# Mixture-of-experts stage: two kinds of experts take turns by column block, three experts of the first kind instead of four

## The chip, the cores and the metric

The kernel runs on one core of one Trainium2 chip. The metric is device time in microseconds (us): the time of one execution. Times of runs without a profile are compared with each other; the trace comes from one profiled execution, whose own time stands beside its span.

## The reference, cut to what matters

The program is two transformer blocks one after the other, 256 tokens of width 1024 in fp32. Around the change stands one mixture-of-experts layer with 8 experts of which each token takes 2:

```python
logits = h @ router_w                      # 256 x 8
top_val, top_idx = top_k(logits, 2)
gates = softmax(top_val)
for each expert e, for the tokens that chose it:
    y = (silu(x @ w1[e]) * (x @ w3[e])) @ w2[e]     # w1, w3: 1024 x 2816, w2: 2816 x 1024
    out[token] += gate * y
```

The weights of one expert are 3 x 1024 x 2816 fp32 numbers, 34.6 MB; all eight are read whole. With the inputs that are used here the routing gives 79 tokens to expert 0 and 109, 96, 58, 48, 42, 41 and 39 to the others in falling order (the reference, evaluated).

## The kernel before, in words

`moe` (L1117) routes the tokens, sorts experts 1 to 7 by their number of tokens (expert 0 keeps the first place, so that its weights can be loaded before the routing is known) and treats the first `NL` = 4 places and the other 4 differently.

**First kind, "three products"** (places 0 to 3): up to 128 tokens each. Every weight chunk is split into a rounded part `hi` (ScalarE, ACT, L325) and the rest `lo` (VectorE, DVE, L326), the tokens likewise, and TensorE (PE) adds three products `hi*hi`, `hi*lo`, `lo*hi` (L1370 for w1 and w3, L1436 for w2).

**Second kind, "plain"** (places 4 to 7): up to 64 tokens each. The weight chunks go to PE as fp32, unsplit (L1387 for w1 and w3, L1450 for w2), two products side by side on the two halves of 64 columns.

Weights come as *chunks* of 1 MB, each as two DMAs of 512 KB on SyncE's (SP's) queue (L310), 33 chunks an expert. The order of the stream is the order of the steps. A **step** `(e, f)` is one column block of an expert: 6 blocks of 512 columns for the first kind (the last has 256), 3 pairs of blocks for the second. `moe_steps` (L58) lists the steps: all of the four first-kind experts, then all of the four plain ones. For each step `moe` (L1501) emits `up(step)` (w1 and w3), inside it between w1 and w3 the transposes `gtrans` of the step before (L1408 or L1417, into PSUM and copied out), and then `down(step before)` (w2). After each one or two chunks `tick` lets a piece of background work come (gathers of the next tokens, L1298 and L1328; `combine` and `combine_plain`, L1456 and L1477, which scatter an expert's result into the residual `hT`) and `pump` loads and splits ahead.

**Buffers.** A chunk needs a place from one of the `home`s (L273). Between 454 and 847 us there are 6 (3 `raw`, 2 `raw2`, 1 `raw3`), and at the start 3 extra ones that are used once (`xbig` twice, `yh`/`yl`). A split chunk gives its place back as soon as the split is emitted; at most `look` = 2 split chunks wait ahead of their use, and `hi` and `lo` have room for 3 chunks. In the plain part the six places of `hi` and `lo` serve as homes as well (L631 to L634), so that there are 12; `may_split` (L344) holds splits back while they do. A plain chunk gives its place back in `done`, after its products (a pair of chunks in `up`, one in `down`).

**PSUM.** Eight banks: 3 for `mm` (the sums `H` and others), 1 `st`, 2 `Y` (the sums of w2), 2 `ac` (all that is short-lived: `gTp` of `gtrans`, gathers, `sc` of the combines).

A second path, `moe_rest` (L1523), handles experts with more tokens than their slots; it runs only where `ovm` (L1221 to L1223) exceeds 128, counting 64 on top for the plain places.

Of the kernel before, what the change touches and what calls it, by code (L numbers as in the profile page):

```python
# [23 lines left out]
NL = 4  # L24
# [33 lines left out]
def moe_steps():  # L58

    return [(e, f) for e in range(NL) for f in range(6)] + [(e, f) for e in range(NL, NE) for f in range(3)]  # L60

# [117 lines left out]
class Prog:  # L179
# [74 lines left out]
    def plan(self):  # L254
# [13 lines left out]

        self.i_plain = self.at_key["m1", NL, 0, 0], self.i_raw2

        self.i_three = self.at_key[down_keys(NL - 1, 5)[-1]]

    def home(self, pool, chunks, tag="raw", ok=lambda i: True):  # L273

        r = dict(pool=pool, free=chunks, tag=tag, ok=ok)
        self.homes.append(r)
        return r
# [16 lines left out]
    def _load(self):  # L294
# [5 lines left out]
        else:  # L300
# [7 lines left out]
            r = [home["pool"].tile([128, n, shape[2]], F32, tag=home["tag"], name=f"raw{i}{h}") for h in range(2)]  # L308
# [316 lines left out]
    def setup(self):  # L625
# [491 lines left out]
    def moe(self, nxt):  # L1117
# [117 lines left out]
        def gates():  # L1235
# [13 lines left out]
            for b in range(2):  # L1249
# [7 lines left out]
        io64 = p.tile([128, 2, 64], F32, name="io64")  # L1257
        nc.gpsimd.iota(io64, pattern=[[0, 2], [1, 64]], base=0, channel_multiplier=0,
                       allow_small_or_imprecise_dtypes=True)
        io64 = io64.rearrange("p a b -> p (a b)")  # L1260


        def slots(es, off=0, io=io8):
            S = p.tile([128, 2, len(es), 128], F32R, tag="ST" if off else "S", name="S", bufs=2 if off else 1)
            for n, e in enumerate(es):
                for b in range(2):
                    if off:
                        nc.vector.tensor_scalar(S[:, b, n], io, float(off), rks[:, b, e:e + 1], op0=OP.add,
                                                op1=OP.is_equal)
                    else:  # L1270
                        nc.vector.tensor_scalar(S[:, b, n], io, rks[:, b, e:e + 1], None, op0=OP.is_equal)
            return S

        def slotsT(S, es, ghl):

            m = len(es)
            ST = p.tile([128, m, T], F32R, tag="ST", name="ST", bufs=2)
# [5 lines left out]
            gs = p.tile([128, m, 2], F32, tag="gs", name="gs", bufs=2)  # L1283
# [10 lines left out]
        first = slots((0, 1))  # L1294
# [3 lines left out]
        def gather(pair):  # L1298
            es = (2 * pair, 2 * pair + 1)
            S = slots(es) if pair else first  # L1300
            last = [None, None]
            if pair % 2:
                g = [self.big("xgh", [128, KD, 2, 128], F32R), self.big("xgl", [128, KD, 2, 128], F32R)]
            else:
                g = [self.xt(n).rearrange("p k (e t) -> p k e t", e=2) for n in ("xgh", "xgl")]
            for i in range(4):
                for s in range(2):
                    ps = self.psum("ac" if s or pair else "mm", "xgp", (128, 2, 256))
                    for j in range(2):
                        for b in range(2):  # L1310
                            k = 2 * i + j
                            nc.tensor.matmul(ps[:, j], xtk[k // 4][:, s, b, 128 * (k % 4):128 * (k % 4) + 128], S[:, b],
                                             start=b == 0, stop=b == 1)
                    o = g[s][:, 2 * i:2 * i + 2].rearrange("p a b c -> p a (b c)")
# [5 lines left out]
            if not pair:  # L1320
                with self.after(*last):
                    ghl.append(gates())
            q = slotsT(S, es, ghl[0])
            for n, e in enumerate(es):
                xg[e] = [x[:, :, n] for x in g]
                sg[e] = q[0][:, n], q[1][:, n]

        def gather_plain():  # L1328

            es = range(NL, NE)  # L1330
            n = len(es)
            S = slots(es, io=io64)
            yield
            g = self.p_x.tile([128, KD, n, 64], F32, tag="X", name="xs")
            for k in range(KD):
                ps = self.ac("xgp", (128, n, 64))
                for s in range(2):
                    for b in range(2):
                        nc.tensor.matmul(ps, xtk[k // 4][:, s, b, 128 * (k % 4):128 * (k % 4) + 128], S[:, b, :, 0:64],
                                         start=s == 0 and b == 0, stop=s == 1 and b == 1)  # L1340
                if k % 2:
# [816 lines left out]
```

## Time and profile before

| | |
|---|---|
| three runs | 1894.77 us median, 1893.84 to 1897.97 |
| the profiled execution | 1895.51 us, its span 1893.7 us |
| granted TensorE clock over the span | 0.985 |
| busy over the span | PE 95%, DVE 66%, ACT 52%, POOL 3% |
| share of the chain that ended last | PE 49%, DMA 18%, DVE 6%, ACT 2% |

The span runs from the first to the last instruction. In what follows the *first stage* is 454 to 847.4 us (experts with three products) and the *second stage* 847.4 to 1184.2 us (plain experts); both are in the middle of the span, behind the first block's mixer and feed-forward layer and ahead of the second block. Busy PE time is modelled, so a stage's PE share is read together with what PE waited for.

### The profile page before, as it was taken

To read this page: it belongs to the slowest core of one execution; us is meant where nothing else is said; L and a number is where in the kernel's file an instruction comes from. 1 tells how busy PE (TensorE), PEld (TensorE's weight loads), DVE (VectorE), ACT (ScalarE), POOL (GpSimd) and SP (SyncE) were. 2 spreads that over 40 slices of the span, in tenths; PEclk is the share of its full clock that TensorE was granted. 3 is DMA by queue.
4 is the path that set the end of the run, shared out by engine and by line. 5 is a ranking of instruction groups with operands and counts; after the bars stand their busy time and mean duration, and the time that the engine had idled before them with its cause. 6 is when DMAs were issued, how large, how long until landed. Compare 5 with 4: busy or idle time off the path is not lost.

```text
span 1893.7 us, 32031 instructions
## 1 busy us (share of the span) xinstructions
PE 1789.7 (95%) x11975; PEld 1474.0 (78%) x11975; DVE 1255.5 (66%) x2216; ACT 975.8 (52%) x1503; POOL 55.4 (3%) x94
## 2 busy tenths in 40 slices
PE   6999999997999999999888988799999999999998
PEld 6999999996888887873232322788899999889997
DVE  6789888687999888971000100786788887676554
ACT  6754336666787777761000000666655556666553
POOL 1010000000000000000000000110100000000000
PEclk9999999998999999999999999899999999999999
DMA  7478886664899999999999999644388884326551
GB/s 254 163 254 323 306 315 211 207 249 161 301 363 328 349 329 354 326 335 392 411 411 411 411 411 411 205 130 143 133 281 318 313 277 145 109 78 200 181 189 54
DMA packets 138547, 508.57 MB, mean 269 GB/s; under 512 B 18192, under 2 KB 18832, under 8 KB 137872
## 3 DMA queue, kind: packets, MB, share of 16 engines
q1 hardware_dynamic: 132768, 497.97, 72.9%
q10 hardware_dynamic: 5616, 8.48, 1.4%
q8 instruction: 96, 1.57, 0.3%
q14 instruction: 67, 0.55, 0.1%
HBM read 505.34 MB, written 1.05 MB: 267 GB/s over the span
## 4 chain that ended last, share of the span: by engine, by line
PE 49%; DMA 18%; DVE 6%; ACT 2%; issue 2%; SPq 0%; DVEq 0%; ACTq 0%
DMA raw<-in_moe_dram 16%; PE H L1370 10%; PE up L406 8%; PE y L603 8%; PE zp L406 5%; PE Y L1436 5%; DVE lo L326 3%; PE H L1387 3%; PE op L406 2%; PE S L1780 1%; DMA adaw<-in_ada_dram 1%; ACT hi L325 1%; PE pg L406 1%; PE pTp L998 1%; PE oT L1814 1%
## 5 line engine op out<-in xcount | busy, mean ns | idle before, releaser
L326 DVE TENSOR_TENSOR lo<-raw,hi 128x1024 fp32r<-128x1024 f32 x580 | 695.1, 1224 | 135.6 <-ACT hi L325 133.1
L325 ACT ACTIVATE hi<-raw 128x1024 fp32r<-128x1024 f32 x580 | 589.8, 1052 | 166.0 <-PE y L603 37.2
L1387 PE MATMUL H<-raw,xs 128*64 128x512 f32 (+1 forms) x768 | 189.6, 574 | 29.9 <-DMA raw<-in_moe_dram 29.8
L603 PE MATMUL y<-glo,hi 128*128 128x256 f32 x688 | 193.4, 281 | 1.3 <-DVE glo L378 1.3
L603 PE MATMUL y<-ghi,hi 128*128 128x256 f32 x688 | 193.2, 281 | 0.6 <-ACT ghi L377 0.6
L603 PE MATMUL y<-ghi,lo 128*128 128x256 f32 x688 | 193.3, 281 | 0.2 <-DVE lo L326 0.2
L1397 DVE SCALAR_TENSOR_TENSOR mg<-H,gs,mg 128x512 f32<-128x512 f32 (+3 forms) x40 | 27.8, 695 | 237.8 <-PE H L1387 138.1
L1387 PEld LDWEIGHTS H<-raw,xs 128*64 128x64 f32 x768 | 61.3, 139 | 146.7 <-issue 76.1
L828 DVE SCALAR_TENSOR_TENSOR adacc<-adaw,cact,adacc 128x768 f32<-128x768 f32 x126 | 130.3, 1034 | 42.4 <-DMA adaw<-in_ada_dram 40.8
L1396 ACT ACTIVATE mg<-H,gs 128x512 f32<-128x512 f32 (+3 forms) x40 | 25.7, 643 | 255.9 <-PE H L1387 239.7
L406 PE MATMUL up<-xhi,hi 128*128 128x258 f32 x512 | 145.6, 285 | 2.4 <-ACT xhi L481 1.8
L1370 PE MATMUL H<-hi,xgh 128*128 128x512 f32 (+1 forms) x384 | 145.8, 380 | 0.0
L406 PE MATMUL up<-xlo,hi 128*128 128x258 f32 x512 | 145.6, 284 | 0.1
L406 PE MATMUL up<-xhi,lo 128*128 128x258 f32 x512 | 145.1, 284 | 0.0
L1370 PE MATMUL H<-lo,xgh 128*128 128x512 f32 (+1 forms) x384 | 144.8, 377 | 0.3
L1370 PE MATMUL H<-hi,xgl 128*128 128x512 f32 (+1 forms) x384 | 143.5, 374 | 0.0
L603 PEld LDWEIGHTS y<-glo,hi 128*128 128x128 f32 x688 | 129.6, 188 | 2.1 <-DVE glo L378 2.1
L603 PEld LDWEIGHTS y<-ghi,hi 128*128 128x128 f32 x688 | 129.3, 188 | 1.2 <-ACT ghi L377 1.2
L603 PEld LDWEIGHTS y<-ghi,lo 128*128 128x128 f32 x688 | 129.6, 188 | 0.6 <-DVE lo L326 0.6
L406 PE MATMUL H<-xhi,hi 128*128 128x256 f32 x352 | 99.3, 283 | 2.3 <-ACT xhi L481 2.3
L406 PE MATMUL H<-xhi,lo 128*128 128x256 f32 x352 | 100.1, 285 | 0.7 <-DVE lo L326 0.7
L1450 PE MATMUL Ys<-raw,gts 128*64 128x512 f32 x352 | 94.4, 606 | 6.6 <-DMA raw<-in_moe_dram 5.9
(552 smaller groups left out, 4017.2 us busy)
## 6 DMA issues: line engine op xcount, KB each, us to landing
raw<-in_moe_dram SPq DMA_DIRECT2D x522, 512.0 KB, 6.4
raw<-in_stream_dram SPq DMA_DIRECT2D x318, 512.0 KB, 4.6
adaw<-in_ada_dram SPq DMA_DIRECT2D x64, 768.0 KB, 6.3
xbig<-in_moe_dram SPq DMA_DIRECT2D x4, 512.0 KB, 5.3
cw1k<-in_cw1k_dram ACTq DMA_DIRECT2D x2, 1024.0 KB, 6.2
cw1v<-in_cw1v_dram ACTq DMA_DIRECT2D x2, 1024.0 KB, 6.7
raw<-in_stream_dram SPq DMA_DIRECT2D x4, 472.0 KB, 4.2
hT<-in_xT_dram SPq DMA_DIRECT2D x4, 256.0 KB, 6.1
```

Of the source, the lines that this page charges most:

```text
L325: nc.scalar.activation(hi, raw, AF.Copy)
L326: nc.vector.tensor_sub(lo, raw, hi.bitcast(F32))
L406: nc.tensor.matmul(ps, p[:, k, j:j + m], q[:, k, :], start=start and n == 0, stop=n == 3 * nk - 1, skip_group_check=True)
L603: self.nc.tensor.matmul(ps, p[:, k, 128 * dt:128 * dt + 128], q[:, k, :], start=f == 0 and n == 0 and dt % 2 == 0, stop=last and n == 5, s ...
L828: nc.vector.scalar_tensor_tensor(acc, w[:, j], self.cact[:, k:k + 1], acc, op0=OP.mult, op1=OP.add)
L998: nc.tensor.transpose(ps[:, o:o + 128], e[:, c:c + 128], self.ident)
L1370: nc.tensor.matmul(ps[:, :n], g[s][:, m // 3], w[:, k], start=m == 0, stop=m == 23, skip_group_check=True)
L1387: nc.tensor.matmul(ps[64 * q:64 * q + 64, :c], g[:, k], x[:, kk], start=k == 0, stop=k == KD - 1, skip_group_check=True)
L1396: nc.scalar.activation(t[z, :c], H[0][z, :c], AF.Silu, scale=gs[z, 1:2])
L1397: nc.vector.scalar_tensor_tensor(t[z, :c], H[1][z, :c], gs[z, 1:2], t[z, :c], op0=OP.mult, op1=OP.mult)
L1436: nc.tensor.matmul(Y[e][q], l[:, kk], r[:, k, 512 * q:512 * q + 512], start=f == 0 and h == 0 and k == 0 and i == 0, stop=f == 5 and k == ...
L1450: nc.tensor.matmul(Y[e][64 * q:64 * q + 64], gt[:, kk, 64 * n:64 * n + 64], w[:, k, 512 * q:512 * q + 512], start=key[2] == 0 and kk == 0, ...
```

## The change

`NL` becomes 3, so places 3 to 7 are plain. `moe_steps` gives first three steps of the first kind and then one plain step and one of the first kind by turns; the last plain step but one is followed by two of the first kind, and a plain step ends the list. There are 18 + 15 = 33 steps (24 + 12 before). The plain tokens are gathered in two groups (three and two experts) that are queued at once after the first step, and each first-kind expert's tokens one expert ahead. The homes in `hi` and `lo` go; `raw3` has two chunks instead of one, and one `xbig` instead of two. PSUM has `Y` = 3 and `ac` = 1; the plain combine uses one `ac` and one `mm` bank instead of two `ac`. A combine is queued when the last step of its expert is done.

```diff
-NL = 4
+NL = 3
...
 def moe_steps():
-    return [(e, f) for e in range(NL) for f in range(6)] + [(e, f) for e in range(NL, NE) for f in range(3)]
+    a = [(e, f) for e in range(NL) for f in range(6)]
+    b = [(e, f) for e in range(NL, NE) for f in range(3)]
+    r, n = a[:3], 3
+    for i, x in enumerate(b):
+        r.append(x)
+        m = 3 + (len(a) - 3) * (i + 1) // (len(b) - 1)
+        r += a[n:m]
+        n = max(n, m)
+    assert r[-1] == b[-1] and len(r) == len(a) + len(b)
+    return r
...
     def may_split(self):
-        if self.i_split not in self.raws or self.plain(self.i_split):
-            return self.i_split in self.raws
-        return len([i for i in self.parts if not self.plain(i)]) < self.look and \
-            not any(x["tag"] != "raw" and x["free"] < x["all"] for x in self.homes if "all" in x)
+        return self.i_split in self.raws and (
+            self.plain(self.i_split) or len([i for i in self.parts if not self.plain(i)]) < self.look)
...
-        for pool, tag in ((self.p_hi, "hi"), (self.p_lo, "lo")):
-
-            self.home(pool, self.look + 1, tag, lambda i: self.i_get > self.i_three + 1 and i < self.i_plain[1] - 6)
-            self.homes[-1]["all"] = self.look + 1
...
-        for _ in range(2):
-            t = self.big("xbig", [128, 2048])
-            self.extra.append([t[:, 0:1024], t[:, 1024:2048]])
+        t = self.big("xbig", [128, 2048])
+        self.extra.append([t[:, 0:1024], t[:, 1024:2048]])
...
-        first = slots((0, 1))
+        first = slots((0,))
...
-        def gather(pair):
-            es = (2 * pair, 2 * pair + 1)
-            S = slots(es) if pair else first
+        def gather(e):
+            S = slots((e,)) if e else first
...
+            g = self.p_x.tile([128, 2, KD, 128], F32R, tag="X", name="xg")
+            for i in range(2):
                 for s in range(2):
...
+                    for j in range(4):
                         for b in range(2):
...
         def gather_plain():
-            es = range(NL, NE)
...
+            g = self.big("xs", [128, KD, NE - NL, 64])
+            for e0 in range(NL, NE, 3):
+                es = range(e0, min(e0 + 3, NE))
...
-                P = [self.ac("sc", (128, 2, T)) for _ in range(2)]
+                P = [self.psum(t, "sc", (128, 2, T)) for t in ("ac", "mm")]
...
             up(e, f, prev)
-            if e < NL and e % 2 and f == 1:
-                self.add(gather(e // 2 + 1) if e < NL - 1 else gather_plain())
+            if n == 0:
+                self.add(gather_plain())
+            if e < NL - 1 and f == 1:
+                self.add(gather(e + 1))
             if prev:
                 down(*prev)
-                if f == 0:
-                    self.add((combine if e <= NL else combine_plain)(e - 1))
+                if prev == (prev[0], 5 if prev[0] < NL else 2):
+                    self.add((combine if prev[0] < NL else combine_plain)(prev[0]))
...
-        with self.more_raw("raw3", "left", 1), self.phase("moe", 2, Y=2, ac=2):
+        with self.more_raw("raw3", "left", 2), self.phase("moe", 1, Y=3, ac=1):
```

## Rows read from the trace of the kernel before

**Rows 1.** The page's 40 slices of the span, 47.3 us each

```profile
PE   6999999997999999999888988799999999999998
...
DMA  7478886664899999999999999644388884326551
GB/s 254 163 254 323 306 315 211 207 249 161 301 363 328 349 329 354 326 335 392 411 411 411 411 411 411 205 130 143 133 281 318 313 277 145 109 78 200 181 189 54
```

**Rows 2.** Busy time by stretch: first stage, second stage, first three steps

```profile
core 0: us, PE busy (x) PEld busy (x) DVE busy (x) ACT busy (x) POOL busy (x), PEclk, DMA share, GB/s
454.00:847.40 393.40, 392.82 (x1895) 322.56 (x1894) 350.35 (x365) 292.89 (x329) 0.12 (x1) 1.00 0.93 333
847.40:1184.20 336.80, 295.92 (x1250) 98.17 (x1248) 32.98 (x52) 16.92 (x25) 0.11 (x1) 0.99 1.02 406
454.00:503.00 49.00, 49.00 (x221) 39.86 (x220) 44.79 (x60) 39.16 (x43) 0.00 (x0) 1.00 0.76 268
```

**Rows 3.** DMA issues of expert weights, 452.2 to 1190 us

```profile
raw<-in_moe_dram SPq DMA_DIRECT2D x506, 512.0 KB, 6.6
```

**Rows 4.** Busy time by stretch: one short stretch of each stage

```profile
650.00:653.00 3.00, 3.00 (x16) 2.45 (x15) 2.24 (x2) 1.10 (x2) 0.00 (x0) 1.00 1.03 419
980.00:1000.00 20.00, 17.88 (x82) 6.96 (x82) 1.42 (x3) 1.15 (x2) 0.00 (x0) 1.00 1.03 411
```

**Rows 5.** SP's queue waits, first stage, then second: us, times, longest

```profile
SPq L310 <- DVE lo L326: 239.3, 235, 10.1
...
SPq L310 <- DMA raw<-in_moe_dram: 182.6, 243, 1.6
```

**Rows 6.** Splits; landing of weight DMAs, first stage, then second

```profile
L326 DVE TENSOR_TENSOR lo<-raw,hi x252: 1209/1219/1228, 443.1 to 845.6; 128x1024 fp32r<-128x1024 f32 x126
...
L325 ACT ACTIVATE hi<-raw x251: 1038/1053/1067, 439.7 to 843.4; 128x1024 fp32r<-128x1024 f32 x126
...
DMA to landing us min/median/max: 3.2/5.3/7.2
...
DMA to landing us min/median/max: 3.5/10.1/11.3
```

**Rows 7.** The page's groups, then groups by line: PE, second kind

```profile
L1387 PE MATMUL H<-raw,xs 128*64 128x512 f32 (+1 forms) x768 | 189.6, 574 | 29.9 <-DMA raw<-in_moe_dram 29.8
...
L1450 PE MATMUL Ys<-raw,gts 128*64 128x512 f32 x352 | 94.4, 606 | 6.6 <-DMA raw<-in_moe_dram 5.9
...
L1490 PE MATMUL sc<-ST,ys 64*128 64x256 f32 x64 | 11.7, 407 | 1.6 <-ACT ys L1482 0.8 <-DVE hT L1493 0.8
...
L1417 PE MATMUL gTp<-ident,mg 128*128 128x128 f32 (+1 forms) x48 | 8.9, 286 | 2.6 <-DVE hT L1493 2.3
```

**Rows 8.** Timeline: products of the second kind around one combine product

```profile
880.06 0.14 PEld L1387 LDWEIGHTS H<-raw,xs 128*64 128x64 f32 x1 [0.29 <-issue]
881.01 0.19 PEld L1472 LDWEIGHTS sc<-ST,yl 128*128 128x128 f32 x1 [0.81 <-issue]
...
881.32 0.20 PEld L1387 LDWEIGHTS H<-raw,xs 128*64 128x64 f32 x4
...
881.80 0.14 PEld L1387 LDWEIGHTS H<-raw,xs 128*64 128x64 f32 x2 [0.28 <-issue]
882.24 0.14 PEld L1387 LDWEIGHTS H<-raw,xs 128*64 128x64 f32 x2 [0.29 <-issue]
```

**Rows 9.** Gather loads, combine additions, gather copies: duration min/median/max

```profile
L1339 PEld LDWEIGHTS xgp<-S,xtk x32: 187/188/192, 779.0 to 803.5; 128*128 128x128 f32 x32
...
L1474 DVE TENSOR_TENSOR hT<-hT,sc x16: 675/680/689, 566.8 to 881.4; 128x512 f32<-128x512 f32 x16
...
L1316 ACT ACTIVATE xgl<-xgp x8: 575/587/598, 451.6 to 601.1; 128x512 fp32r<-128x512 f32 x8
```

**Rows 10.** Timeline: the first product of the experts and the last

```profile
454.10 0.19 PEld L1370 LDWEIGHTS H<-hi,xgh 128*128 128x128 f32 x1
...
1183.58 1.08 PE L1450 MATMUL Ys<-raw,gts 128*64 128x512 f32 x4 [0.20 <-DMA raw<-in_moe_dram]
```

More of the change, by code (lines that the diff above doesn't have):

```diff
@@ L267, in plan, with home @@
         self.i_raw2 = self.at_key["pple", 1]
[L269 to L275, printed above, removed]
+    def home(self, pool, chunks, ok=lambda i: True):
+        r = dict(pool=pool, free=chunks, ok=ok)
         self.homes.append(r)
@@ L307, in _load @@
             self.at_home[i] = home
-            r = [home["pool"].tile([128, n, shape[2]], F32, tag=home["tag"], name=f"raw{i}{h}") for h in range(2)]
+            r = [home["pool"].tile([128, n, shape[2]], F32, tag="raw", name=f"raw{i}{h}") for h in range(2)]
         for h in range(2):
@@ L1254, in gates, with slots @@
             return ghl
[L1257 to L1264, printed above, removed]
+        def slots(es, off=0, plain=False):
+            S = p.tile([128, 2, len(es), 128], F32R, tag="ST" if off else "Ss" if plain else "S", name="S",
+                       bufs=2 if off else 1)
             for n, e in enumerate(es):
@@ L1267, in slots, with slotsT @@
                     if off:
[L1268 removed]
+                        nc.vector.tensor_scalar(S[:, b, n], io8, float(off), rks[:, b, e:e + 1], op0=OP.add,
                                                 op1=OP.is_equal)
+                    elif plain:
+                        nc.vector.tensor_scalar(S[:, b, n].rearrange("p (a t) -> p a t", a=2),
+                                                io8[:, None, 0:64].to_broadcast([128, 2, 64]), rks[:, b, e:e + 1],
+                                                None, op0=OP.is_equal)
                     else:
[L1271 removed]
+                        nc.vector.tensor_scalar(S[:, b, n], io8, rks[:, b, e:e + 1], None, op0=OP.is_equal)
             return S
[L1274 removed]
+        def slotsT(S, es, ghl, z=""):
             m = len(es)
[L1277 removed]
+            ST = p.tile([128, m, T], F32R, tag="ST" + z, name="ST", bufs=1 if z else 2)
             pg = self.psum("st", "gsp", (128, m, 2, 2))
@@ L1292, in slotsT @@
             return ST, gs
-        first = slots((0, 1))
+        first = slots((0,))
         self.moe_rest(xtk, cni, eidi, slots, slotsT, gates)
         xg, sg, ghl = {}, {}, []
-        def gather(pair):
-            es = (2 * pair, 2 * pair + 1)
-            S = slots(es) if pair else first
+        def gather(e):
+            S = slots((e,)) if e else first
             last = [None, None]
[L1302 to L1306, printed above, removed]
+            g = self.p_x.tile([128, 2, KD, 128], F32R, tag="X", name="xg")
+            for i in range(2):
                 for s in range(2):
-                    ps = self.psum("ac" if s or pair else "mm", "xgp", (128, 2, 256))
-                    for j in range(2):
+                    ps = self.psum("ac" if s or e else "mm", "xgp", (128, 4, 128))
+                    for j in range(4):
                         for b in range(2):
-                            k = 2 * i + j
-                            nc.tensor.matmul(ps[:, j], xtk[k // 4][:, s, b, 128 * (k % 4):128 * (k % 4) + 128], S[:, b],
+                            nc.tensor.matmul(ps[:, j], xtk[i][:, s, b, 128 * j:128 * j + 128], S[:, b, 0],
                                              start=b == 0, stop=b == 1)
-                    o = g[s][:, 2 * i:2 * i + 2].rearrange("p a b c -> p a (b c)")
+                    o = g[:, s, 4 * i:4 * i + 4]
                     if s:
@@ L1319, in gather @@
                     yield
-            if not pair:
+            if not e:
                 with self.after(*last):
                     ghl.append(gates())
[L1323 to L1326, printed above, removed]
+            ST, gs = slotsT(S, (e,), ghl[0])
+            xg[e] = g[:, 0], g[:, 1]
+            sg[e] = ST[:, 0], gs[:, 0]
         def gather_plain():
-            es = range(NL, NE)
@@ L1331, in gather_plain @@
[L1331 to L1341, printed above, removed]
-                    nc.scalar.activation(g[:, k], ps, AF.Copy)
-                else:
-                    nc.vector.tensor_copy(g[:, k], ps)
-                yield
@@ L1346, in gather_plain @@
-            q = slotsT(S, es, ghl[0])
-            for n, e in enumerate(es):
-                xg[e] = g[:, :, n]
-                sg[e] = q[0][:, n], q[1][:, n]
+            g = self.big("xs", [128, KD, NE - NL, 64])
+            for e0 in range(NL, NE, 3):
+                es = range(e0, min(e0 + 3, NE))
+                n = len(es)
+                S = slots(es, plain=True)
+                yield
+                for k in range(KD):
+                    ps = self.ac("xgp", (128, n, 64))
+                    for s in range(2):
+                        for b in range(2):
+                            nc.tensor.matmul(ps, xtk[k // 4][:, s, b, 128 * (k % 4):128 * (k % 4) + 128],
+                                             S[:, b, :, 0:64], start=s == 0 and b == 0, stop=s == 1 and b == 1)
+                    o = g[:, k, e0 - NL:e0 - NL + n]
+                    if k % 2:
+                        nc.scalar.activation(o, ps, AF.Copy)
+                        yield
+                    else:
+                        nc.vector.tensor_copy(o, ps)
+                q = slotsT(S, es, ghl[0], f"s{e0}")
+                for m, e in enumerate(es):
+                    xg[e] = g[:, :, e - NL]
+                    sg[e] = q[0][:, m], q[1][:, m]
```

4 lines of the change are left out of this document (2 added, 2 removed).

## The prediction, made before the change was run

> **What bounds the kernel now.** I read the page's slices first, then busy time by stretch, then the waits of SP's queue, then single rows. The slices [rows 1] show two halves of one layer that are limited by different things: in slices 11 to 18 PE is full and the stream moves 326 to 363 GB/s; in slices 19 to 24 it moves 411 GB/s and PE has gaps. The stretches [rows 2] say it exactly. First stage: PE is busy 392.8 of 393.4 us and the DMA moves 333 GB/s. Second stage: 406 GB/s, PE 295.9 of 336.8 us. What SP's queue waits for agrees [rows 5]: in the first stage for `lo` (a place in the ring comes free when the split is done, 235 times), in the second for an earlier weight DMA (243 times). So four experts go at PE's pace, 393.4/4 = 98.35 us each, and four at the stream's, 336.8/4 = 84.2 us each; each half leaves unused what the other lacks. First product to last [rows 10]: 1183.58 + 1.08 - 454.10 = 730.6 us. This stretch is all that I let the change move; the rest of the program keeps its instructions.
>
> **The stream's floor.** After 452.2 us, 506 DMAs of 512 KB are still to come [rows 3], and the same number after the change: 22 are loaded ahead in both versions (six homes and three extras with two split chunks before; seven and two with two after). At its best the stream moves 411 GB/s [rows 4], that is 524288/411e9 = 1.276 us a DMA, 2.55 us a chunk. 506 x 1.276 = 645.5 us. One short stretch of the first stage reaches 419 GB/s [rows 4], so the splits of ACT and DVE beside it don't slow the stream; I take 411 throughout.
>
> **Does PE fit under it?** First kind: 3 x 98.35 = 295.1 us, gathers and combines included. Plain: the 768 + 352 instructions of w1, w3 and w2 [rows 7] are 280 an expert, and where nothing holds them two start every 0.43 us (881.80 to 882.24) [rows 8]: 60.2 us; transposes 8.9/4 = 2.2 and combine 11.7/4 = 2.9 [rows 7]: 65.3 us, times 5 = 326.6. New are the changes between the two kinds of product: 14 plain steps stand ahead of first-kind ones, so some 28 changes. One combine product between plain ones [rows 8] moves the next plain loads from 880.06 to 881.32, 1.26 us where 0.43 is usual; without the product itself (about 0.1) that is 0.36 us for each of two changes, and I take 0.4: 11 us. PE's sum is 633 us, below the stream's. By the Trainium skill, page TensorEngine Tiling (Array Packing), section Tiling Modes, a change of tiling mode drains TensorE, which speaks against taking turns; the page gives no price. The trace agrees as far as a weight load waits 0.81 us there [rows 8], and at 0.81 for each change PE's sum would be 645 us, level with the stream's floor.
>
> **Part by part, in time.**
> *Start.* The first three steps are still all of the first kind. There the stream moves 268 GB/s in 49 us [rows 2], so 49 x (1 - 268/411) = 17.0 us of stream are lost, as now. A ring with seven places for six lets one more chunk through: -2.6. The first gather handles one expert for two, four PSUM copies fewer, shared by ACT and DVE: two of 0.59 us [rows 9], -1.2. New in this start are the plain gather and the next expert's gather, 96 products; at 0.188 us a weight load [rows 9] they are 18 us if all fall before the first plain step, nothing if they slide behind it, where PE has room. I take 10, the middle.
> *The turns.* Per turn a plain step is 12 chunks, 30.6 us of stream and about 22 of PE; a step of the first kind is 6 chunks, 15.3 us of stream and 16 to 18 of PE. The ring lends the stream at most one or two chunks in the second, and gets them back in the first. Cover is seven places; if it ran out, the stream would wait for PE. The homes in `hi` and `lo` that go I cost at nothing: in the second stage landing takes 10.1 us in the median [rows 6] while SP waits for earlier DMAs, so some eight DMAs, four chunks, are under way, and seven places hold these and the pair in use. What is late next is the hand-over from plain to split chunks: the split is emitted when its chunk is only on its way, its place is given on at once, and the DMA that gets it waits on SP's queue, with all DMAs behind it, until `lo` is done. After landing that takes ACT 1.05 and DVE 1.22 us [rows 6]; a new DMA needs some 1.9 us to flow (shortest landing 3.2 [rows 6] less its own 1.28); one chunk of 2.55 us is under way meanwhile. Gap: 1.05 + 1.22 + 1.9 - 2.55 = 1.6 us, 14 times, 22.7 us at worst by this row. If the place comes from a plain chunk used earlier there is none. I take half: 11.3.
> *Queued behind the new waits.* ACT and DVE work in order. Behind a split that waits for its chunk stand the copy of `gTp`, the activation of `H` and the combine's additions; PE needs the first of these only one or two chunks later, and has 682 - 633 = 49 us to wait in (sum below), 3.5 us a turn.
> *Banks.* One `ac` bank for two: `gTp` 33 times, combines 22, gathers about 30, in all some 85 uses; each can make PE wait for an addition of 0.68 us [rows 9] and at worst one `lo` of 1.22 [rows 6] in front of it, 1.9 us, 161 us in all; at best nothing, since 85 uses in 690 us leave 8 us between them. The first stage, with DVE at 89% [rows 2], kept PE full with two. I take it within PE's 49 us, so nothing; this is the term that I trust least.
> *End.* The combine of the last first-kind expert now falls into the last plain step: four additions of 0.68 us [rows 9] on DVE, next to 7.7 us of stream; I take 2 us, between 0 and 2.7 and what precedes them.
>
> Sum: 645.5 + 17.0 - 2.6 - 1.2 + 10 + 11.3 + 2 = 682.0 us for 730.6, a gain of 48.6. From the profiled execution's 1895.5 us: 1846.9, I say **1847**. That execution stands 0.7 us above the median of the runs, less than the sum can tell. A measurement of this kernel tells about 0.2%, 3.8 us, from no change.
>
> **The rivals.**
> *All of it hidden:* no gaps at the hand-over, gathers behind the start: 682.0 - 21.3 - 2 = 658.7, 1824 us. For it: 419 GB/s beside splits [rows 4]. Against: seven places.
> *The single bank sets the pace:* at 0.8 us for each of 85 uses PE's sum is 633 + 68 = 701, a gain of 29.6: 1866 us. For it: DVE's queue is full in steps of the first kind [rows 2]. The Trainium skill, page Perfetto Trace Analysis, section Matmuls, has independent groups of products rotate through PSUM banks so that the copying out lies beside the next products, and one bank can't rotate; no row here shows one bank alone.
> *Turns hide nothing:* first-kind steps keep PE's 98.35 us an expert and plain ones the stream's 84.2; then only one expert changes sides: 3 x 98.35 + 5 x 84.2 = 716.1, and with the start's 10 and the end's 2 less 1.2 it is 727: 1892 us, no change within 0.2%.
> *Slower: splits block the queues of ACT and DVE.* The split of the next first-kind chunks is emitted up to seven places ahead, behind plain chunks still to land. ACT then stands before it, the copy of `gTp` or a combine's addition stays behind, the one `ac` bank stays taken, and PE, in order, waits at the next transposes with plain chunks lying ready. Place: inside `up` of each plain step. Price: up to 7 x 2.55 = 17.9 us a turn. It decides from (730.6 - 633)/14 = 7 us a turn on; at 9 PE's sum is 759, 1924 us. For it: in the first stage ACT and DVE hardly waited for a DMA because the stream was ahead, and here it will not be. Against: PE falling behind puts the stream ahead again, and the waits shrink.
> *Not what it says:* the path for overfull experts would run 13 blocks of 33 chunks, over 1000 us; the fourth place has 58 tokens for 64, so no.
>
> **How the numbers follow.** Forecast 0.48 (1836 to 1858); all hidden 0.13; bank 0.15; nothing hidden 0.10, half of it within 0.2%; slower 0.12; 0.02 for the rest, faster than now. Faster: 0.48 + 0.13 + 0.15 + 0.06 + 0.02 = 0.84; same 0.04; slower 0.12. The range must leave out at most 2 in 10: I leave out slower, half of nothing hidden, and the fastest corner: 1822 to 1888. The forecast's own is 1836 to 1858.
>
> **What would show it.** Right: GB/s over the whole stretch even, near 390, no slice of 411 and none of 340; from first to last product about 682 us; SP's waits a mixture of `lo` and earlier DMAs; PE with gaps at the first chunk of each first-kind run, about 3 us. Wrong: PE waits on `ac` users (`gTp`, `sc`, gathers) of over 50 us in sum (bank), ACT's `hi` waiting long for DMA while PE waits for ACT or DVE (blocked queues), or slices that still go between 340 and 411 GB/s (nothing hidden).

## The result: 0.7% slower, and the profile after

The changed kernel takes 1911.82 us (median of 7 runs, 1906.17 to 1915.19); beside it the kernel before takes 1897.80 us (7 runs, 1893.01 to 1902.52). The ratio is 1.0069, 95% interval 1.0047 to 1.009. The forecast of 1847 us and its range (1822 to 1888) both missed, and the sign was wrong.

The profiled execution has a span of 1910.2 us. First the slices of its page, to hold against [rows 1]: 47.8 us each.

```profile
PE   7999999998999999989999889899999999999998
...
DMA  7478886564589998999999999643378884326551
GB/s 271 155 263 306 297 312 205 178 237 167 182 345 414 398 362 354 372 386 414 373 364 381 353 413 376 227 144 133 129 271 315 310 281 151 111 78 199 177 186 57
```

The two halves of [rows 1] are gone, so the turns do what they say; but in place of an even 390 GB/s there are slices of 413 and 414 between slices of 353 to 398, and a slice of 182 at the start. (By the prediction's own signs, slices that still go between 340 and 411 meant "turns hide nothing", which would have taken 1892 us; the time is longer than that too.) The timeline gives 461.7 us for the first expert product, 527.1 for the first plain one and 1199.9 for the start of the last: 738.2 us where it was 1184.1 - 454.1 = 730.0 [rows 10] and where the forecast had 682. Ahead of the stage this execution was 7.6 us later; the kernels of this study, whose code there is the same or nearly so, came to their first product between 453.0 and 464.1 us, so I compare stretches, not clock times. Of the 16.5 us by which the two profiled executions differ, the stretch explains 8.2; since each kernel has one trace, it is not shown how much of the 7.6 us is the change's doing. Busy time by stretch, the start and the turns (columns as in [rows 2]):

```profile
461.70:527.10 65.40, 63.92 (x327) 49.75 (x327) 44.06 (x71) 35.79 (x46) 0.00 (x0) 0.97 0.55 189
527.10:1199.90 672.80, 623.88 (x2725) 321.45 (x2726) 260.85 (x274) 213.78 (x236) 0.23 (x2) 1.00 0.96 380
```

The last column tells where the time is. Against 411 GB/s the start loses 65.4 x (1 - 189/411) = 35.3 us of stream, the turns lose 672.8 x (1 - 380/411) = 50.7 us. What SP's queue waited for in the turns, 530 to 1150 us (total, times, longest), beside [rows 5]:

```profile
SPq L315 <- DMA raw<-in_moe_dram: 196.6, 261, 5.4
SPq L315 <- DVE lo L331: 81.6, 45, 6.9
SPq L315 <- PE H L1381: 70.0, 42, 4.3
SPq L315 <- PE Ys L1444: 23.4, 36, 3.1
```

A single wait for `lo` is up to 6.9 us long, though one `lo` takes 1.2 us. One such hand-over from a plain step to a step of the first kind, in stretches of 2 us from 806 to 818:

```profile
806.00:808.00 2.00, 2.00 (x12) 0.62 (x9) 0.00 (x0) 1.33 (x2) 0.00 (x0) 1.00 1.02 418
808.00:810.00 2.00, 1.09 (x5) 0.15 (x2) 0.75 (x1) 1.83 (x2) 0.00 (x0) 1.00 0.26 107
810.00:812.00 2.00, 1.11 (x6) 0.68 (x6) 1.32 (x2) 1.06 (x2) 0.00 (x0) 1.00 0.00 0
812.00:814.00 2.00, 1.44 (x6) 1.22 (x7) 2.00 (x3) 0.00 (x0) 0.00 (x0) 1.00 0.26 49
814.00:816.00 2.00, 2.00 (x10) 1.59 (x10) 1.91 (x2) 0.22 (x1) 0.00 (x0) 1.00 0.96 268
816.00:818.00 2.00, 2.00 (x10) 1.43 (x8) 1.13 (x1) 0.83 (x1) 0.00 (x0) 1.00 0.90 295
```

The stream stands still. ACT's timeline there:

```profile
806.51 1.06 ACT L330 ACTIVATE hi<-raw 128x1024 fp32r<-128x1024 f32 x1 [4.78 <-DMA raw<-in_moe_dram]
807.73 1.06 ACT L330 ACTIVATE hi<-raw 128x1024 fp32r<-128x1024 f32 x1 [0.16 <-DMA raw<-in_moe_dram]
```

DVE's:

```profile
809.18 0.75 DVE L1391 SCALAR_TENSOR_TENSOR mg<-H,gs,mg 128x512 f32<-128x512 f32 x1 [6.39 <-PE H L1381]
810.68 0.69 DVE L1413 COPY gts<-gTp 128x512 f32<-128x512 f32 x1 [0.75 <-PE gTp L1411]
811.29 4.62 DVE L331 TENSOR_TENSOR lo<-raw,hi 128x1024 fp32r<-128x1024 f32 x4
```

And what SP's queue waited for longest, 798 to 826 us:

```profile
SPq L315 <- DVE lo L331: 6.6, 2, 6.0
...
SPq L315 <- PE H L1381: 5.3, 2, 4.2
```

ACT has the first half's `hi` ready at 807.57, as soon as the chunk has landed. DVE could do `lo` then, but in the order of its instructions `mg` comes first, the multiplication of the plain step that waits for that step's last product: DVE was idle for 6.39 us in front of it. Then it waits for the transposes and copies `gTp`; only at 811.29 do four `lo` run back to back. Both halves' `lo` are done some 3.6 us later than they could be (two of them end about 813.6; the second `hi` ends at 808.79, with 1.2 us for its `lo` 810.0). All that time the place of a chunk that has landed is not free, the DMA that was given it stands at the head of SP's queue, and every DMA behind it stands too. The hole has a second part. Just before, SP had waited 4.2 us for `H`, that is for the place of a plain chunk; between 798.0 and 812.5 us it issued two DMAs only, so few were still under way when the wait for `lo` began. In the trace the same pair of waits, first for `H` and then for `lo`, stands ahead of five of the six deep holes (not of that near 1034). About half of the fourteen hand-overs show such a hole (near 714, 760, 810, 988, 1034, 1082, and milder ones near 668 and 945); in the others the next place came from a plain chunk used earlier.

### The profile page after: what moved, and what is told of

Same layout as the page of the kernel before. It is cut to its first block, busy times and chain, and to the rows that moved or that the text cites. A ratio compares the mean times of both kernels' runs of the same rounds, so it can differ in the third digit from the quotient of the medians.

```text
span 1910.2 us, 31506 instructions
## 1 busy us (share of the span) xinstructions
PE 1799.8 (94%) x11889; PEld 1432.0 (75%) x11889; DVE 1177.9 (62%) x2150; ACT 913.6 (48%) x1428; POOL 53.3 (3%) x93
## 3 DMA queue, kind: packets, MB, share of 16 engines
HBM read 505.34 MB, written 1.05 MB: 265 GB/s over the span
## 4 chain that ended last, share of the span: by engine, by line
PE 50%; DMA 13%; DVE 8%; issue 2%; ACT 2%; SPq 0%; DVEq 0%; ACTq 0%
DMA raw<-in_moe_dram 9%; PE H L1381 8%; PE H L1364 8%; PE up L409 6%; PE zp L409 5%; PE y L606 5%; DVE lo L331 4%; PE Ys L1444 4%; DMA adaw<-in_ada_dram 4%; PE Y L1430 3%; PE op L409 2%; PE S L1776 2%; ACT hi L330 1%; DVE adacc L827 1%; PE pTp L997 1%
## 5 line engine op out<-in xcount | busy, mean ns | idle before, releaser
L331 DVE TENSOR_TENSOR lo<-raw,hi 128x1024 fp32r<-128x1024 f32 x516 | 620.2, 1227 | 149.6 <-ACT hi L330 147.6
L330 ACT ACTIVATE hi<-raw 128x1024 fp32r<-128x1024 f32 x516 | 530.6, 1053 | 257.5 <-DMA raw<-in_moe_dram 112.6
L1381 PE MATMUL H<-raw,xs 128*64 128x512 f32 (+1 forms) x960 | 225.5, 563 | 9.5 <-DMA raw<-in_moe_dram 9.4
L1381 PEld LDWEIGHTS H<-raw,xs 128*64 128x64 f32 x960 | 75.4, 136 | 141.0 <-issue 112.1
L1364 PE MATMUL H<-hi,xg 128*128 128x512 f32 (+1 forms) x576 | 175.8, 381 | 0.8 <-ACT hi L330 0.8
L1364 PEld LDWEIGHTS H<-hi,xg 128*128 128x128 f32 x576 | 105.6, 190 | 22.3 <-ACT hi L330 3.8
L1364 PE MATMUL H<-lo,xg 128*128 128x512 f32 (+1 forms) x288 | 113.8, 395 | 4.0 <-DVE lo L331 3.8
L1444 PE MATMUL Ys<-raw,gts 128*64 128x512 f32 x440 | 113.6, 601 | 0.5 <-DVE gts L1415 0.5
L409 PE MATMUL H<-xlo,hi 128*128 128x256 f32 x352 | 99.4, 282 | 0.0
```

What stands on the lines that cost most here:

```text
L330: nc.scalar.activation(hi, raw, AF.Copy)
L331: nc.vector.tensor_sub(lo, raw, hi.bitcast(F32))
L409: nc.tensor.matmul(ps, p[:, k, j:j + m], q[:, k, :], start=start and n == 0, stop=n == 3 * nk - 1, skip_group_check=True)
L1364: nc.tensor.matmul(ps[:, :n], g[s][:, m // 3], w[:, k], start=m == 0, stop=m == 23, skip_group_check=True)
L1381: nc.tensor.matmul(ps[64 * q:64 * q + 64, :c], g[:, k], x[:, kk], start=k == 0, stop=k == KD - 1, skip_group_check=True)
L1444: nc.tensor.matmul(Y[e][64 * q:64 * q + 64], gt[:, kk, 64 * n:64 * n + 64], w[:, k, 512 * q:512 * q + 512], start=key[2] == 0 and kk == 0, ...
```

## Experiments

The theory that they test first: **this hand-over** cost the gain. Rivals: the single `ac` bank, a ring that is too small, a start that is too long, and TensorE's own time. All kernels are the changed one with the edit named. The table is for all of them: the median, the ratio to the kernel before (run beside it) with its interval, the time from the start of the first expert product to that of the last, and the stream's rate from 530 to 1150 us, in the profiled execution. The last two columns are of one execution each, which can lie some us from the median (`seq`: 1883.6 us profiled, 1889.6 median; the last row: 1899.0 and 1893.8), so differences of a few us in them tell little.

| kernel | us | ratio, 95% | first to last product | GB/s |
|---|---|---|---|---|
| before | 1897.8 | 1 | 730.0 | 372 |
| changed | 1911.8 | 1.0069 (1.0047 to 1.0090) | 738.2 | 382 |
| keep: place kept until used | 1884.1 | 0.9947 (0.9928 to 0.9966) | 723.3 | 393 |
| lofirst: `lo` ahead of `mg` | 1881.3 | 0.9933 (0.9909 to 0.9957) | 712.3 | 400 |
| gtst: `gTp` to another bank | 1911.3 | 1.0092 (1.0066 to 1.0117) | 749.0 | 376 |
| seq: no turns | 1889.6 | 0.9970 (0.9954 to 0.9987) | 726.2 | 386 |
| start2: two steps at the start | 1914.9 | 1.0091 (1.0064 to 1.0118) | 746.3 | 371 |
| lofirst, start2 | 1893.6 | 0.9995 (0.9976 to 1.0015) | 721.5 | 388 |
| lofirst, later gather | 1889.7 | 0.9956 (0.9938 to 0.9975) | 716.2 | 394 |
| **lofirst, keep** | 1865.0 | 0.9843 (0.9817 to 0.9869) | 694.1 | 410 |
| both, later gathers | 1866.9 | 0.9839 (0.9815 to 0.9864) | 697.5 | 402 |
| both, start2 | 1866.3 | 0.9835 (0.9811 to 0.9859) | 694.7 | 405 |
| both, later gathers, start2 | 1863.8 | 0.9825 (0.9797 to 0.9853) | 697.5 | 400 |
| both, ring of six | 1875.8 | 0.9879 (0.9848 to 0.9910) | 704.8 | 404 |
| both, later gathers, start2, no third term | 1854.4 | 0.9791 (0.9770 to 0.9811) | 681.4 | 406 |
| both, no third term | 1853.8 | 0.9778 (0.9752 to 0.9803) | 688.5 | 408 |
| changed, no third term | 1893.8 | 0.9992 (0.9974 to 1.0009) | 727.5 | 385 |

### Two cures of the hand-over, each alone

**Keep.** The place of a split chunk is given back when TensorE's products take the chunk.

```diff
             self.parts[i] = tuple(Halves([x[n] for x in hl]) for n in range(2))
-            self.leave(i)
+            if not self.i_first < i < self.i_raw2:
+                self.leave(i)
...
         if self.plain(i):
             self.got.append(i)
+        elif self.i_first < i < self.i_raw2:
+            self.leave(i)
```

> Edit: of the chunks that are split during the turns, the place in the ring is given back when TensorE's products take the chunk, no longer at the moment the split is emitted; so SP's queue never stands before a lo on DVE that itself stands behind other work. Hand-over theory (the changed kernel loses some 46 us of stream in the turns because the place of a split chunk just landed waits for its lo, which waits behind mg and the copy of gTp): the holes of 0 to 100 GB/s after plain steps go, SP's waits for lo fall from 114.6 us to near those of the start, first product to last 739 becomes 695 to 720, time 1868 to 1893. Ring theory (seven places are too few): a place is held longer, so 1912 to 1930. Single-bank theory: no change, 1905 to 1916. Start theory (the loss is all ahead of the first plain step): no change.

**Lofirst.** DVE's `mg` is put behind the `lo` of the next split chunk (`self.los` holds the last `lo` of each chunk).

```diff
+            first = [self.los[i] for i in sorted(self.los) if i >= self.i_get][:1] if e >= NL else []
...
-                nc.vector.scalar_tensor_tensor(t[z, :c], H[1][z, :c], gs[z, 1:2], t[z, :c], op0=OP.mult, op1=OP.mult)
+                with self.after(*first):
+                    nc.vector.scalar_tensor_tensor(t[z, :c], H[1][z, :c], gs[z, 1:2], t[z, :c], op0=OP.mult, op1=OP.mult)
```

> Edit: on DVE the multiplication mg of a plain step is emitted behind the lo of the next split chunk, not ahead of it. Hand-over theory: lo runs about 1.2 us after its hi, not 4 to 7 us later, so most of the holes shrink from 4 to 6 us to 1 to 2: 1875 to 1900. Blocked-queue theory (the forecast's slower rival: a split that waits for its chunk holds up the plain step's own work): now mg stands behind a lo that waits for a DMA, TensorE's w2 products start later, so slower than 1912, up to 1935. Single-bank theory: no change, 1905 to 1916.

Both are faster than the changed kernel, by 27.7 and 30.5 us, and their times are inside what the hand-over theory expected; the ring theory (slower) and the blocked-queue theory (slower) expected the opposite. With keep the holes are gone (from 530 to 1150 us no 2 us are below 160 GB/s), but two of its expectations miss: the stretch is 723.3 us, 3 above its range, and SP's waits for `lo` do not fall to those of the start. The same kind of place with the `lo` first, on DVE:

```profile
746.05 2.56 DVE L332 TENSOR_TENSOR lo<-raw,hi 128x1024 fp32r<-128x1024 f32 x2 [4.58 <-ACT hi L331]
750.62 0.74 DVE L1395 SCALAR_TENSOR_TENSOR mg<-H,gs,mg 64x512 f32<-64x512 f32 x1 [2.01 <-PE H L1383]
```

DVE's idle time now ends with `hi`, not with the plain product, and two `lo` run 4.6 us ahead of `mg`. The stream from 746 to 748 us:

```profile
746.00:748.00 2.00, 2.00 (x11) 0.84 (x11) 1.84 (x2) 1.53 (x3) 0.00 (x0) 1.00 0.48 190
```

190 GB/s where it was 0: no hole here, but a dip (the deepest of this kind left is 88 GB/s, near 964 us), since the DMA at the head of SP's queue still waits for the `lo` of a chunk that has only just landed. That is what keep takes away; but with keep alone `lo` stays late. What SP, and what TensorE's w2 products waited for with keep, 530 to 1150 us:

```profile
SPq L316 <- DVE lo L332: 73.1, 89, 5.6
...
PE Y L1434 <- DVE lo L332: 17.4, 13, 1.5
```

In the changed kernel these were 81.6 and 17.5 us. Each leaves what the other cures.

### The bank alone, and no turns

**Gtst.** The transposes of `gTp` go to the bank `st`.

```diff
-            ps = self.psum("gT", "gTp", (128, 4, 128))
+            ps = self.psum("st", "gTp", (128, 4, 128))
```

> Edit: the transposes of gTp go to the PSUM bank st and not to the single bank ac that combines and gathers share; nothing else. Single-bank theory (PE waits for a bank that DVE has not yet emptied): faster by 15 us or more, below 1897. Hand-over theory: within 4 us of the changed kernel, 1907 to 1916, with the same holes in the stream.

1911.3 us: nothing. Some 33 of the 85 uses leave the bank and the time stays, so it did not set the pace. (Combines and gathers were left on `ac`; but in the changed kernel from 530 to 1150 us TensorE waited only 3.1 us for `hT`'s additions ahead of `gTp`, and 3.9 ahead of the plain combines, for `ys` and `gtl`, which are no readers of the bank.)

**Seq.** Three experts of the first kind, then five plain ones.

```diff
+    return a + b
     r, n = a[:3], 3
```

> Edit: no turns; the three experts of the first kind one after the other, then the five plain ones; all else as in the changed kernel. By the rows of the kernel before, 3 x 98.35 + 5 x 84.2 = 716 us for 730.6, with some 12 us more in the start and the end: 1892 less or more 8. Hand-over theory: as there is one hand-over and not fourteen, it is faster than the changed kernel, by 10 to 25 us (1887 to 1902), and its stream shows no holes. Start theory: it loses the same in its first steps as the changed kernel, and the stretch after them is not shorter than the changed kernel's: 1905 to 1915. If turns hide something in spite of the holes, it is slower than 1915.

1889.6 us, 22.2 less than with the turns and 0.3% below the kernel before: one expert changing sides is worth what the rival "turns hide nothing" worked out (1892), and the turns as written cost more than they hid. The range of the hand-over theory holds; that of the start theory does not. Its one hand-over, at 764 us, has one hole (0 and 131 GB/s in two stretches of 2 us); no other is below 150 GB/s from 526 to 1150 us.

### The start

**Start2.** Two steps of the first kind stand ahead of the first plain one.

```diff
-    r, n = a[:3], 3
+    r, n = a[:2], 2
...
-        m = 3 + (len(a) - 3) * (i + 1) // (len(b) - 1)
+        m = 2 + (len(a) - 2) * (i + 1) // (len(b) - 1)
...
+        key, shape, blocks = self.ch[i]
+        if blocks is None and key[1] and not self.eid:
+            return False
```

> Edit: two steps of the first kind, not three, stand ahead of the first plain step; a chunk of an expert is not loaded before its number is known. Nothing else. Start theory (from the first product to the first plain one 65.4 us pass at some 200 GB/s, so each 16.5 us step ahead of it costs about half of itself in stream): the start becomes about 49 us and the total 6 to 12 us shorter than the changed kernel, 1899 to 1906. If the stream that is not lost in the start is lost again at the hand-overs, no change: 1908 to 1915. Hand-over theory alone says no change.

1914.9 us, no gain, where the start theory gave 1899 to 1906, though 27.3 us and not 65.4 pass until the first plain product. SP's queue from 455 to 530 us tells why:

```profile
SPq L318 <- PE STp L1291: 18.0, 1, 18.0
SPq L318 <- PE H L1384: 11.1, 8, 2.9
```

One wait of 18.0 us (stream 21 GB/s from 490 to 500 us): the first plain chunks are used, and then TensorE does w2 products of the second step and gathers before the next plain ones (492.4 to 502.3 us in its timeline), so the places don't come back. The work only moved, as I read it. With the `lo` first as well, and with the gather of the second expert handed out later:

```diff
-            if e < NL - 1 and f == 1:
+            if e < NL - 1 and f == 4:
                 self.add(gather(e + 1))
```

> Edit: the lo of the next split chunk ahead of mg, as before, and two steps instead of three at the start. If the loss at the start and that at the hand-overs add up: 6 to 12 us below the run with the lo first, 1869 to 1875. If the stretch is then bound by TensorE, whose busy time in it is near 695 us, the start doesn't matter: 1878 to 1884.

> Edit: lo first, and the gather of the second expert is handed out from its fifth step's place on (f = 4), not in the second step; it leaves the start and falls into the turns. Start theory, with the gathers part of it: 32 products of 0.188 us leave the start, 6 us of TensorE there, about half of it stream: 1876 to 1880. If its DVE and ACT copies then add to the hand-overs: 1882 to 1890.

1893.6 and 1889.7 us, both slower than lofirst alone. The first misses both of its ranges: the turns' rate falls from 400 to 388 GB/s, and why a shorter start costs 12 us there is not settled. The second is as the last of its two cases: the start is 4 us shorter (64.6 to 60.6), the turns 7.9 us longer.

### Both cures

> Edit: both cures of the hand-over at once: lo first, and the place of a split chunk is given back only when TensorE takes the chunk. If both cure the same loss: no better than either alone, 1878 to 1886. If lo first leaves holes (dips to 200 GB/s remain after plain steps) that the later return takes away: 1862 to 1876. If the later return now costs places for nothing: 1884 to 1895.

1865.0 us, 46.8 less than the changed kernel and 1.6% below the kernel before. They add up in part: alone they gave 27.7 and 30.5 us, 58.2 together. SP's waits from 530 to 1150 us, against those of the changed kernel above:

```profile
SPq L317 <- DMA raw<-in_moe_dram: 254.5, 355, 2.2
SPq L317 <- PE H L1387: 58.8, 61, 3.5
SPq L317 <- PE Ys L1452: 32.6, 50, 3.4
SPq L317 <- DVE lo L333: 16.4, 30, 2.1
```

`lo` falls from 81.6 to 16.4 us, its longest wait from 6.9 to 2.1, and what SP mostly waits for is the stream itself. The start, and the turns:

```profile
460.80:525.50 64.70, 63.22 (x326) 49.19 (x325) 44.07 (x71) 35.81 (x46) 0.00 (x0) 0.98 0.57 190
525.50:1154.90 629.40, 614.59 (x2723) 321.76 (x2724) 258.77 (x272) 214.53 (x237) 0.23 (x2) 1.00 1.01 407
```

The turns go from 672.8 to 629.4 us, the start stays as it was. So the late places were 43 us of the 57 by which the forecast's stretch was missed, and the turns now lose only 629.4 x (1 - 407/411) = 6.1 us of stream, where the forecast allowed 13.3. What is still missing to 682 us comes from the start and from the amount of data (below).

### What is left at 694 us

Three shorter starts on top of both cures. **Late** is the gather at f = 4 and this:

```diff
             if n == 0:
-                self.add(gather_plain())
+                self.add(gather_plain((NL,)))
+            if (e, f) == (NL + 1, 0):
+                self.add(gather_plain((NL + 3,)))
```

> Edit: both cures, and two gathers leave the start: that of the second expert goes to its predecessor's fifth step (f = 4), and that of the last two plain experts into the first step of the second plain expert. Start theory: 64 products of 0.188 us, 12 us of TensorE, leave the 64.7 us ahead of the first plain step; at about half the stream's rate there, 4 to 8 us: 1857 to 1861. If gathers among the turns open holes in the stream again: 1865 to 1876.

> Edit: both cures, and two steps instead of three at the start. If the start was worth nothing only because the stream won there was lost again at the hand-overs, then without these it counts: 6 to 12 us less than both cures, 1853 to 1859. If the gathers and the second step's w2 products merely move behind the first plain chunks, whose places then stay taken: 1863 to 1874.

> Edit: both cures, the two gathers later, and two steps at the start. If both parts of the start count and add up: 1848 to 1855, where the forecast was. If only one does: 1856 to 1862. If neither: 1863 to 1876.

1866.9, 1866.3 and 1863.8 us: none can be told from 1865.0, and each is in the slowest of its ranges. The last of them, from the first product to 510 us and from there to the last:

```profile
455.40:510.00 54.60, 54.60 (x248) 35.66 (x249) 32.97 (x53) 27.19 (x34) 0.00 (x0) 0.95 0.64 225
510.00:1152.90 642.90, 630.47 (x2802) 338.34 (x2801) 270.03 (x291) 220.74 (x248) 0.23 (x2) 1.00 1.01 400
```

TensorE is busy in 685.1 of 697.5 us. The stream that is won at the start (225 for 190 GB/s) is lost later (400 for 407). That suggests TensorE as the next limit; so a kernel with less work for it. **No third term** leaves out the product of x's low part with w's high part in w1 and w3; all weights are still loaded and split.

```diff
-                            for s, w in ((0, whi), (0, wlo), (1, whi)):
+                            for s, w in ((0, whi), (0, wlo)):
...
-                                nc.tensor.matmul(ps[:, :n], g[s][:, m // 3], w[:, k], start=m == 0,
-                                                 stop=m == 23, skip_group_check=True)
+                                nc.tensor.matmul(ps[:, :n], g[s][:, m // 2], w[:, k], start=m == 0,
+                                                 stop=m == 15, skip_group_check=True)
```

> Edit: as the run with both cures, the later gathers and two steps at the start, and the products of the first kind of w1 and w3 leave out the third of their three terms (x's low part times w's high part): 288 products of 0.23 us, 67 us of TensorE, are gone; every weight is still loaded and split. TensorE theory (with the holes cured TensorE sets the stage, its sum is near 680 us): the stream takes over, its dips between 530 and 1150 us (22.9 us of stream) go, and the time falls by 12 to 25 us, 1840 to 1852. Stream theory (the dips come from places and queues): 1858 to 1864.

> Edit: both cures, the start as in the changed kernel, and without the third term in w1 and w3. The three steps of the start lose 48 products, 11 us. Stream and TensorE theory agree on the turns here, since the stream already runs at 410 of 415 GB/s in them; what is won is the shorter start: 1850 to 1858.

> Edit: the changed kernel without the third term in w1 and w3; 67 us of TensorE less, nothing else. Hand-over theory: the holes come from the order on DVE and stay; only the start is shorter by 11 us and the plain steps begin a little earlier: 1893 to 1906. TensorE theory (the loss is TensorE's own time): falls by 30 us or more, below 1882.

The first of them, from its first product to its last:

```profile
461.70:1143.10 681.40, 644.44 (x2759) 321.90 (x2761) 301.82 (x343) 246.03 (x282) 0.23 (x2) 0.99 0.99 395
```

1854.4 us lies between the ranges of the two theories. TensorE's busy time falls from 685.1 to 644.4 us, by 41 and not by 67 (48 of the 288 products are only 256 columns wide; what else is missing stays open). The stretch falls by 16.1 us and the time by 9.4, and part of the dips stays (282 to 369 GB/s from 630 to 680 us, where gathers fall into the turns), so TensorE was a limit, but not alone. 1853.8 us is in its range, not quite by its account: the start is 15.3 us shorter (64.7 to 49.4), the turns are 9.7 us longer (629.4 to 639.1). And in the changed kernel the holes don't care how much TensorE has to do. Its groups by tile (duration min/median/max in ns, first and last start), and one of its holes:

```profile
L1364 PE MATMUL H<-hi,xg x288: 278/394/735, 456.6 to 1150.3; 128*128 128x512 f32 x120, 128*128 128x256 f32 x24
L1444 PE MATMUL Ys<-raw,gts x440: 592/592/644, 556.1 to 1184.1; 128*64 128x512 f32 x147
...
1070.00:1072.00 2.00, 0.55 (x3) 0.12 (x2) 2.00 (x3) 0.14 (x1) 0.00 (x0) 1.00 0.00 0
```

Its first plain product comes at 505.7, so the start shrinks from 65.4 to 49.1 us, but the turns take 1184.1 - 505.7 = 678.4 us (672.8 with the term), at 385 GB/s from 530 to 1150 us, though TensorE's busy time in them falls from 623.9 to 606.0. Six holes are there as before (near 705, 750, 798, 975, 1020 and 1070 us). It ends at 1893.8 us, at the fast edge of what the hand-over theory gave it, 12 us above the 1882 of the other. It is 18.0 us faster than the changed kernel, and its start is 16.3 us shorter: where work was dropped and not moved, the start seems to count.

**Ring of six.** `more_raw("raw3", "left", 1)` for 2, with both cures.

> Edit: both cures, with six places in the ring instead of seven. The forecast counted a seventh place as 2.6 us in the start and the turns as covered by seven. If that is so and six cover them too: 1866 to 1870. If the places are what lends the stream time in the steps of the first kind (one place is 2.55 us of stream in each of fourteen turns): 1880 to 1900.

1875.8 us, between its two ranges: one place is worth 10.8 us. In the profile 1.8 us of it are in the start (66.5 for 64.7) and 8.9 in the turns (638.3 for 629.4), 0.6 us a turn. The seven places were not more than enough; whether an eighth would gain was not run.

## Why the prediction was wrong

*The bound of the kernel before, and the idea:* right. With the hand-over cured the stream runs at 407 GB/s over the turns, beside the splits, and the kernel takes 1865 us. That this is next to the 1866 of the rival "bank" is chance: its cause did not show.

*The stream's floor:* right in its rate (slices of 414), a little low in its amount. The stretch moves 730.0 us x 367 GB/s = 268 MB before and 738.2 x 363 = 268 MB after; at 411 that is 652 us and not 645.5. That is data of some five DMAs more than the 506, 6.5 us: six loads of the later stage's weights (`in_stream_dram`) are issued in the same stretch.

*Start:* 35.3 us of stream are lost where the steps of the sum gave 17.0 - 2.6 - 1.2 + 10 = 23.2: 12.1 too few. The term of 10 us for the gathers took the middle; the gathers don't slide behind the first plain step: all 96 products run ahead of it (64 of L1332, and 32 of the 33 of L1305, from 461.7 to 527.1 us). But moving the work did not win this loss back: six kernels have a shorter start with the same work, and none of them is faster than its companion beyond the spread.

*Hand-over:* this is the step that failed. The prediction named the place, the waiting DMA and the half of the turns in which the place comes from a plain chunk, and priced it at 1.6 us x 14, half taken, 11.3 us; with the end's 2 that is 13.3, and the turns lost 50.7. It gave `lo` its own time after landing, as if DVE were idle and free: "After landing that takes ACT 1.05 and DVE 1.22 us". DVE was idle, but not free: an instruction of the plain step stood in front. The rival "splits block the queues" had the queues in the other order, a split that waits with the plain step's work behind it. It asked which work a waiting split delays, and not which work delays a split. Forcing the order that the rival feared (lofirst) made the kernel faster. So the sign came out as in that rival, by another mechanism. For a place that "comes from a plain chunk used earlier" it counted no gap; in the trace SP waits for such a place too (`H`, 4.2 us) just before it waits for `lo`, so that the second wait finds few DMAs under way.

The three terms give 6.5 + 12.1 + 37.4 = 56.0 of the 56.8 us between 682.0 and 738.8 (738.2, and 0.6 for the last product itself). The rest of the miss in the profiled execution (1912.0 for 1846.9) is outside the stretch, 7.6 us of it ahead, where the prediction had put nothing.

*TensorE's sum:* too low, though it cost nothing as long as the holes were there. 633 us were worked out; with both cures it is busy 677.8 of 694.1 us. The gathers' 10 us were in the start's term, not in this sum. And there are more changes between the kinds: the timeline of the run with both cures has 29 from a first-kind product to a plain one and 28 back, where 28 in all were counted, because the products of two neighbouring steps are interleaved. One pair of changes there:

```profile
890.78 0.28 PE L1370 MATMUL H<-lo,xg 128*128 128x256 f32 x1
890.90 0.40 PE L1370 MATMUL H<-hi,xg 128*128 128x256 f32 x2
891.23 1.07 PE L1452 MATMUL Ys<-raw,gts 128*64 128x512 f32 x2
892.23 0.39 PE L1370 MATMUL H<-lo,xg 128*128 128x256 f32 x1
```

From 890.90 to 892.23 are 1.33 us for two narrow products (0.12 each, by the starts before) and one plain pair (0.43 [rows 8]): 0.66 us too long for two changes, so the 0.4 for one was near and their number was not: 57 x 0.33 = 19 us for 11, an estimate from this one pair. By the Trainium skill, page TensorEngine Tiling (Array Packing), section Tiling Modes, a change of mode drains the engine; this row agrees, with 0.33 us. These two parts make 18 of the 45 us; where the rest of TensorE's sum comes from stays open.

*Bank:* its term, nothing, was right as far as tried (`gTp` moved, no change). *Ring:* "Cover is seven places" holds; the seventh is worth 0.6 us a turn, and in the start 1.8 us where 2.6 were forecast. *End:* not separated. *"Turns hide nothing":* its 1892 us is what the kernel without turns takes, 1889.6.

## What to carry to other kernels

A buffer's place comes back when the engine that frees it reaches that instruction, so price the return by what stands in front of it in that engine's order, not by the instruction's own time; an idle engine in the profile may be an engine that waits in front of the work you need. Where DMAs wait in order on one queue, one place that comes back late stops all of them; give a place on only when its release no longer hangs on work of another step. And when two limits are planned to hide each other, add up both in full: here the cure of the stream's holes brought the stretch (694.1 us) to within some 16 us of TensorE's busy time in it (677.8), and moving work out of the start then won nothing.

## What the runs showed that was not expected

The stream went from 418 to 0 GB/s within 4 us, although some eight DMAs are usually under way (an estimate: the median landing in the changed kernel's stage is 9.8 us after the issue, and 1.276 us is one DMA's share of the stream). By that estimate the wait of 6.0 us for `lo` alone would not have emptied the queue; the wait for `H` just before it had already thinned it. After the stop the stream ran at 268 to 295 GB/s for another 4 us before it was back near 400: here a hole cost more than the wait that made it.
